# New prices in the planner's clock and an earlier high part of the weights, in a hybrid encoder layer on one Trainium2 core

## The chip, the cores and the metric

The kernel runs on one core of one Trainium2 chip. The time is device microseconds of one execution of the whole layer, from inputs in device memory to outputs in device memory. TensorE (PE) multiplies matrices, VectorE (DVE), ScalarE (ACT) and GpSimd (POOL) work on elements, and SyncE (SP) issues most of the transfers. Each engine executes its own list of instructions in the order in which the program wrote them, and waits on semaphores where it needs another engine's result.

## The reference

The layer is applied to two request groups, one sequence of 512 tokens and one of 1024, with one shared set of weights in float32 (width 1024). It has three sublayers, each with a normalization before and after, and shift, scale and gate from a conditioning vector:

```
x <- x + 1/2 * gate1 * norm(SwiGLU_1(mod(norm(x))))            # 1024 -> 2816 -> 1024
x <- x + gate2 * norm([pool_mixer(z_pool) | rwkv7_mixer(z_rwkv)] @ W_out),  z = mod(norm(x)) @ W_in
x <- x + 1/2 * gate3 * norm(SwiGLU_2(mod(norm(x))))
```

The RWKV mixer has 8 heads of 64, and runs a linear recurrence over the tokens in both directions:

```
S = S * decay_t + (S @ -kk_t) b_t^T + v_t k_t^T        # 64 x 64 a head, b = kk * a
y_t = S @ r_t
```

The two directions are added, normalized by head, given a bonus term and multiplied by a gate.

## The kernel before

**Blocks.** The 1536 tokens are three blocks of 512: blocks 0 and 1 are the long sequence, block 2 the short one. Activations stand with features on the 128 partitions and tokens along the free dimension.

**Dense layers.** A product in float32 accuracy is made of three products in the faster format float32r: weights and activations are each split into a high part and a low part, and `mm3` issues high x high, high x low and low x high. In names of the profile `whi` and `wlo` are parts of weights, `hh`/`hl` and `gh`/`gl` of activations, and `u`, `v`, `y` are accumulators in PSUM. One weight tile is 128 x 512 elements and serves 12 such products of 512 columns. The class `WStream` (line 483) feeds the tiles: `load` issues a transfer from device memory into one of five buffers `wraw`; `split` makes the high part (a copy by ACT) and the low part (a subtraction by POOL or DVE); `get`, called for each tile that is used, has tile i + 3 split and tile i + 8 loaded. While the scan runs (`scanning` is not empty), DVE makes every low part; otherwise POOL makes most of them.

**The scan.** The recurrence is computed in chunks of 64 tokens. Twelve macro steps, eight for the long sequence (group 1 of the code) and four for the short one, each hold two groups of four chunks in two directions (`gi` is 0 or 1). `scan_prep` makes decays and masked chunk matrices. `scan_inv` inverts triangular chunk matrices, for `gi` 0 by 62 dependent small DVE operations and for `gi` 1 by 62 dependent small POOL operations on the tile `XN`; before them stand two transposes on DVE (`XN<-MU`), and after them three (`MU<-XN` twice, `MU<-MU`), followed by 16 products of 32 x 32 on TensorE (`sM<-MU`), a copy by ACT and 16 more. The two inversions exclude each other. `scan_state` carries the state chunk by chunk, for each direction in three steps of a few products (`sb<-SBD,AR` and `sb<-MU`; `sb<-XN,MU`; `sb<-MU,BKt`, `sb<-AR,SBD` and `sb<-MU`), with copies by ACT between them and an update of the state `SBD` by DVE at the end. `scan_post` normalizes what is done.

**What runs beside what.** The main process goes through feed-forward 1 of blocks 0, 1 and 2, the input projections and the output projections, then feed-forward 2. The scan of the long sequence runs beside feed-forward 1 of block 2 (`mainC`) and what follows. The output projection of block 0 (`wout_gen`) needs the flag `("m", 1)`, which says that the long sequence's scan is done. Between layers, `post_gen` and `prenorm` (normalization after and before a sublayer, column tile by column tile, on DVE, ACT and POOL) make the inputs of the next dense layer. The projections of the pooled half (`wpool_gen`) are placed between them.

**What sets the order.** All of this is written as generators. The program that builds the kernel runs them one step at a time and notes an estimated clock (`Estimate`): for each engine the time at which it would be free, for each piece of each tile the time at which it would be ready. Every call on an engine passes through `Queue` (which is why all instructions have line L161 in the profile), and `Estimate.op` adds a price in nanoseconds to the engine's time. It prices the instruction by engine, operation and number n of elements a partition (or columns of a product, with k rows and m columns of the stationary operand), and holds the result ready for other engines `lat` later. `run_until` then picks, at TensorE's estimated time, the ready process of the smallest priority number. A process that yields `WAIT` is ready again some time after the result of its last instruction would be ready elsewhere, `AFTER_STATE` for priority 0 and `AFTER_OTHER` for the rest; one that yields `CHAIN` (the inversions) is ready `CHAIN_LEAD` before that result; one that yields `PIPE` (columns of `post_gen` and `prenorm`), 300 after it. The estimate exists only while the kernel is built. What remains of it is the order of the instructions on each engine. The choice of POOL or DVE for some operations (`pick`, `split`) is made by the same clock.

Of the kernel before, what the change touches and what calls it, by code (L numbers as in the profile page):

```python
# [10 lines left out]
F32R = mybir.dt.float32r  # L11
I32 = mybir.dt.int32
AF = mybir.ActivationFunctionType
# [4 lines left out]
P = 128  # L18
# [4 lines left out]
TB = 512  # L23
# [5 lines left out]
L2_EPS = 1e-12  # L29
WINDOWS = (2, 4, 8, 16)  # L30
PAD = 8
AFTER_STATE = 200
AFTER_OTHER = 400
CHAIN_LEAD = 300
PRIO_INV, PRIO_PREP, PRIO_POST, PRIO_NORM, PRIO_ZFIN = -0.5, -0.5, 0.8, 0, 0.9
POOL_LATE = 4000
OUT_AT = 7
# [4 lines left out]
class Estimate:  # L42
# [3 lines left out]
    def __init__(self):  # L46
        self.free = dict.fromkeys("VSGTY", 0.0)
        self.seen, self.rings, self.whole = {}, {}, set()
        self.last, self.table, self.moved = 0.0, None, 0.0

    def ring(self, t, key, bufs, whole=False):
        r = self.rings.setdefault(key, [])
# [34 lines left out]
    def op(self, e, name, args, kw):  # L87
        aps = [x for x in list(args) + list(kw.values()) if hasattr(x, "tensor") and hasattr(x, "offset")]
        out = kw.get("out", aps[0])
        n = 1  # L90
        for k in out.shape[1:]:
            n *= k
        t0 = self.free[e]
        boxes = [(self.box(x), x is out) for x in aps]
        for (nm_, p0, p1, f0, f1), w in boxes:
            for q in self.seen.get(nm_, ()):
                if q[0] < p1 and p0 < q[1] and q[2] < f1 and f0 < q[3]:
                    t = max(q[4], q[5] if w else 0.0)
                    t0 = max(t0, t + (0.0 if e == "T" else 130.0) if e == q[6] else t + q[7])
        lat = 150.0  # L100
        if name == "dma_start":
            cost, t = 60.0, max(t0 + 1700.0, self.moved)
            self.moved = t + n * out.shape[0] / 90.0
            lat = self.moved + 1400.0 - t0 - cost
        elif e == "S":
            f = str(args[2]) if len(args) > 2 else ""
            cost = 85 + 0.833 * n + (190 if hasattr(kw.get("scale"), "tensor") else 0)
            t = "e" if "Exp" in f else "s" if ("Silu" in f or "Tanh" in f) else self.table
            if t != self.table:
                cost += 1280  # L110
                self.table = t
        elif e == "V":
            cost = 65 + 1.04 * n + (60 if name == "scalar_tensor_tensor" else 0)
        elif e == "G":
            cost = {"memset": 50 + n, "tensor_scalar": 217 + 1.05 * n, "tensor_copy": 200 + 3 * n}.get(name, 100 + 2.2 * n)
        else:
            l = args[1]
            k, m = l.shape[0], 1
            for q in l.shape[1:]:
                m *= q  # L120
            if name == "transpose":
                cost = 125.0
            elif "32r" in str(l.dtype):
                cost = n / 2.35
            elif m <= 4:
                cost = 0.57 * n
            elif n >= 128:
                cost = 2.1 * n
            elif n >= 64:
                cost = 125.0 if k <= 64 else 190.0 if m > 64 else 78.0  # L130
            else:
                cost = 130.0 if m > 64 else 55.0
            lat = 200.0
        self.t0_ = t0
        t1 = t0 + cost
        self.free[e] = t1
        if name == "dma_start":
            e = "D"
        else:
            self.last = max(self.last, t1 + lat)  # L140
        for (nm_, p0, p1, f0, f1), w in boxes:
            l = self.seen.setdefault(nm_, [])
            if w:
                l[:] = [q for q in l if not (p0 <= q[0] and q[1] <= p1 and f0 <= q[2] and q[3] <= f1)]
                l.append((p0, p1, f0, f1, t1, 0.0, e, lat))
            else:
                l.append((p0, p1, f0, f1, 0.0, t1, e, lat))
            if len(l) > 48:
                del l[:16]
# [23 lines left out]
def encoder_kernel(ctx, tc, x_prompt, x_sample, c_prompt, c_sample, ada_w, ada_b, n1_pre, n1_post,  # L173
# [5 lines left out]
    V, S, G, T, SY = (Queue(est, *q) for q in (("V", nc.vector), ("S", nc.scalar), ("G", nc.gpsimd), ("T", nc.tensor),  # L179
                                               ("Y", nc.sync)))  # L180
# [3 lines left out]
    def nm(s):  # L184
        uid[0] += 1
        return f"{s}{uid[0]}"
# [15 lines left out]
    def mt(shape, tag, bufs, dt=F32, pool=None):  # L202
        return est.ring((pool or mp).tile(shape, dt, name=nm(tag), tag=tag, bufs=bufs), (id(pool), tag), bufs)
# [4 lines left out]
    class Proc:  # L208
        def __init__(self, gen, prio):
            self.gen, self.prio, self.ready, self.cond = gen, prio, est.free["T"], None  # L210
# [6 lines left out]
    def run_until(stop):  # L217
# [3 lines left out]
        while not stop():  # L221
# [27 lines left out]
            elif r == CHAIN:  # L249
                p_.ready = est.last - CHAIN_LEAD  # L250
            else:
                p_.ready = max(est.last + (AFTER_STATE if p_.prio == 0 else AFTER_OTHER), est.free["T"] + (0.0 if r == WAIT else r))

# [229 lines left out]
    class WStream:  # L483
        def __init__(self, items):
            self.items, self.raw, self.out = items, {}, {}
            self.i, self.nl, self.ns = 0, 0, 0

        def load(self, upto):
            while self.nl <= min(upto, len(self.items) - 1):
# [6 lines left out]
        def split(self, upto):  # L496
            while self.ns <= min(upto, len(self.items) - 1):
                self.load(self.ns)
                t = self.raw.pop(self.ns)
                wh = mt([P, TB], "whi", 5, F32R)  # L500
                wl = mt([P, TB], "wlo", 5, F32R)
                S.activation(wh, t, AF.Copy)
                now = est.free["T"]
                g_, v_ = max(now, est.free["G"]) + 1200, max(now, est.free["V"]) + 600
                E = G if not scanning and (g_ < now + POOL_LATE or g_ < v_) else V
                E.tensor_tensor(wl, t, wh.bitcast(F32), ALU.subtract)
                self.out[self.ns] = (wh, wl)
                self.ns += 1

        def get(self):  # L510
            i = self.i
            self.i += 1
            self.split(i + 3)
            self.load(i + 8)
            return self.out.pop(i)

    def cols(w, c0):
# [1111 lines left out]
```

## Time and profile before

| what | value |
|---|---|
| median of 3 runs | 3786.08 us (3785.57 to 3786.62) |
| profiled execution, its time | 3780.28 us |
| its span (first to last instruction) | 3778.3 us |
| TensorE busy | 3593.2 us, 95% of the span |
| VectorE busy | 1999.0 us, 53% |
| ScalarE busy | 1424.1 us, 38% |
| GpSimd busy | 1410.4 us, 37% |
| mean granted TensorE clock | 0.956 |
| read from device memory | 367.23 MB |

A row of a timeline gives start, duration, engine, operation, the tile written and the tiles read, shapes, count and, in brackets, idle time of the engine before it and what ended that. A row of a table by windows gives a stretch of time, then the busy time and the count of each engine in it, then the granted TensorE clock, the share of time in which the transfer engines were busy, and GB/s. A row of waits gives who waited for whom, microseconds in total, how often, and the longest.

### The profile page before, as it was taken

The page shows a single profiled execution, that of the slowest core. Times are in us where ns is not written, and L with a number is a line of the kernel's source. Part 1 is how long each engine was busy: PE and PEld are TensorE (multiplying, and loading weights), DVE is VectorE, ACT ScalarE, POOL GpSimd, SP SyncE. Part 2 cuts the span into 40 slices and gives each one's busy share as a digit, 9 for nine tenths or more (in the row PEclk, how much of TensorE's full clock was granted, in tenths as well). Part 3 has the DMA queues.
Part 4 walks back from the last instruction along what each step waited for, and adds up shares of the span by engine and source line. Part 5 has one row for each costly group of instructions (what it writes and reads, how often), then busy time and mean ns, then how long its engine had stood idle before and what let it go on. Part 6 is the DMA issues. An engine that isn't in the chain of part 4 may idle for free. (4 is left out here: it accounts for less than half of the span.)

```text
span 3778.3 us, 53665 instructions
## 1 busy us (share of the span) xinstructions
PE 3593.2 (95%) x19579; PEld 2703.6 (72%) x19579; DVE 1999.0 (53%) x3801; ACT 1424.1 (38%) x2776; POOL 1410.4 (37%) x1716
## 2 busy tenths in 40 slices
PE   7999999998999999999899989799999999999998
PEld 4667878876676767666666666567787778877886
DVE  3128362237237778776777776778448622242223
ACT  3324342225335434344345433343334432234222
POOL 2333444443132222234234233432344344444444
PEclk8999999998999999999889978599999999999999
DMA  7655343334344322222324343222254333334332
GB/s 274 235 181 169 91 154 92 99 90 134 123 128 126 93 67 88 82 71 87 117 76 122 96 137 105 74 73 77 87 159 151 103 115 98 93 109 132 94 95 78
DMA packets 557980, 432.11 MB, mean 114 GB/s; under 512 B 27029, under 2 KB 511572, under 8 KB 553620
## 3 DMA queue, kind: packets, MB, share of 16 engines
q1 hardware_dynamic: 524900, 379.90, 32.8%
q10 hardware_dynamic: 32816, 48.78, 4.1%
q8 instruction: 155, 2.54, 0.3%
q14 instruction: 109, 0.89, 0.1%
HBM read 367.23 MB, written 61.34 MB: 113 GB/s over the span
## 5 line engine op out<-in xcount | busy, mean ns | idle before, releaser
L161 POOL TENSOR_TENSOR wlo<-wraw,whi 128x512 fp32r<-128x512 f32 x672 | 892.6, 1346 | 1294.2 <-ACT whi L161 866.5
L161 DVE TENSOR_TENSOR y<-y,y 128x512 f32<-128x512 f32 x480 | 327.2, 684 | 848.9 <-PE y L161 847.9
L161 ACT ACTIVATE whi<-wraw 128x512 fp32r<-128x512 f32 x938 | 559.2, 622 | 181.6 <-PE v L161 139.7
L161 PE MATMUL u<-hh,whi 128*128 128x512 f32 x1392 | 568.2, 408 | 10.2 <-ACT zraw L161 4.0
L161 PE MATMUL u<-hl,whi 128*128 128x512 f32 x1392 | 564.3, 405 | 14.1 <-POOL hl L161 7.4
L161 PE MATMUL v<-hh,whi 128*128 128x512 f32 x1392 | 562.4, 404 | 12.8 <-ACT hh L161 7.6
L161 PE MATMUL u<-hh,wlo 128*128 128x512 f32 x1392 | 567.0, 407 | 0.1
L161 PE MATMUL v<-hl,whi 128*128 128x512 f32 x1392 | 561.0, 403 | 1.0 <-DVE hl L161 1.0
L161 PE MATMUL v<-hh,wlo 128*128 128x512 f32 x1392 | 560.7, 403 | 0.0
L161 PE MATMUL y<-gh,whi 128*128 128x512 f32 x1056 | 425.6, 403 | 12.8 <-DVE y L161 10.8
L161 PE MATMUL y<-gl,whi 128*128 128x512 f32 x1056 | 422.7, 400 | 0.2 <-DVE gl L161 0.2
L161 PE MATMUL y<-gh,wlo 128*128 128x512 f32 x1056 | 422.2, 400 | 0.0
L161 POOL TENSOR_TENSOR XN<-XN 64x126 f32<-64x126 f32 (+22 forms) x744 | 322.4, 433 | 93.6 <-DVE XN L161 18.5
L161 PEld LDWEIGHTS u<-hl,whi 128*128 128x128 f32 x1392 | 266.6, 191 | 81.5 <-DVE hl L161 12.6
L161 ACT ACTIVATE gh<-s 128x512 fp32r<-128x512 f32 x132 | 83.3, 631 | 639.3 <-DVE s L161 639.3
L161 PEld LDWEIGHTS u<-hh,whi 128*128 128x128 f32 x1392 | 266.3, 191 | 80.9 <-issue 7.7
L161 PEld LDWEIGHTS v<-hh,whi 128*128 128x128 f32 x1392 | 264.2, 190 | 82.9 <-ACT hh L161 11.3
L161 PEld LDWEIGHTS u<-hh,wlo 128*128 128x128 f32 x1392 | 266.3, 191 | 68.8 <-issue 9.5
L161 PEld LDWEIGHTS v<-hl,whi 128*128 128x128 f32 x1392 | 264.4, 190 | 66.3 <-issue 4.9
L161 PEld LDWEIGHTS v<-hh,wlo 128*128 128x128 f32 x1392 | 264.8, 190 | 62.9 <-issue 5.9
L161 DVE TENSOR_TENSOR wlo<-wraw,whi 128x512 fp32r<-128x512 f32 x266 | 206.4, 781 | 150.6 <-ACT whi L161 149.8
L161 PEld LDWEIGHTS y<-gh,whi 128*128 128x128 f32 x1056 | 199.9, 189 | 67.2 <-DVE y L161 12.0
(252 smaller groups left out, 4504.6 us busy)
## 6 DMA issues: line engine op xcount, KB each, us to landing
wraw<-in_f_w_dram SPq DMA_DIRECT2D x792, 256.0 KB
ada<-in_ada_w_dram SPq DMA_DIRECT2D x32, 1024.0 KB
wraw<-in_w_in_dram SPq DMA_DIRECT2D x98, 256.0 KB
xk<-xs ACTq DMA_DIRECT2D x96, 256.0 KB
xs<-y ACTq DMA_DIRECT2D x48, 256.0 KB
wraw<-in_w_out_dram SPq DMA_DIRECT2D x48, 256.0 KB
in_k<-zk SPq DMA_DIRECT2D x48, 128.0 KB
in_kk<-zkk SPq DMA_DIRECT2D x48, 128.0 KB
```

The source lines that it names most:

```text
L161: return f(*args, **kw)
```

## The change

It has two parts. In the first, the estimate's prices, its latency and three constants of the order are replaced. The latency from one engine to another goes from 150 to 380 (from TensorE, from 200 to 170), the extra charge of 130 for a dependence on the same engine goes, prices depend on more kinds of instruction, and TensorE gets a charge of 95 where a small product follows a dense one. In the second, `WStream` makes the high part in a function of its own: `get` has the high part of tile i + 3, the low part of tile i + 2 and the load of tile i + 7 issued.

```diff
-AFTER_STATE = 200
-AFTER_OTHER = 400
-CHAIN_LEAD = 300
+AFTER_STATE = 0
+AFTER_OTHER = 150
+CHAIN_LEAD = 500
...
-                    t0 = max(t0, t + (0.0 if e == "T" else 130.0) if e == q[6] else t + q[7])
-        lat = 150.0
+                    t0 = max(t0, t if e == q[6] else t + q[7])
+        lat = 380.0
...
-            cost = 85 + 0.833 * n + (190 if hasattr(kw.get("scale"), "tensor") else 0)
+            cost = 150 + 0.9 * n + (100 if hasattr(kw.get("scale"), "tensor") or hasattr(kw.get("bias"), "tensor") else 0)
...
-            cost = 65 + 1.04 * n + (60 if name == "scalar_tensor_tensor" else 0)
+            if name == "transpose":
+                cost = 100 + 1.8 * n
+            elif name == "tensor_tensor_scan":
+                cost = 150 + 2.0 * n
+            elif name == "tensor_scalar" or name == "tensor_copy":
+                cost = 150 + 0.75 * n
+            else:
+                cost = 150 + 1.04 * n + (60 if name == "scalar_tensor_tensor" and n <= 64 else 0)
         elif e == "G":
-            cost = {"memset": 50 + n, "tensor_scalar": 217 + 1.05 * n, "tensor_copy": 200 + 3 * n}.get(name, 100 + 2.2 * n)
+            cost = {"memset": 50 + n, "tensor_scalar": 217 + 1.05 * n, "tensor_copy": 200 + 3 * n}.get(
+                name, 200 + (2.1 if n > 256 else 1.65) * n)
...
             if name == "transpose":
-                cost = 125.0
+                cost = 120.0
             elif "32r" in str(l.dtype):
-                cost = n / 2.35
+                cost = 232.0 * n / 512
             elif m <= 4:
                 cost = 0.57 * n
+            elif n >= 256:
+                cost = (2.05 if k > 64 else 1.5) * n
             elif n >= 128:
-                cost = 2.1 * n
+                cost = 410.0 if k > 64 else 158.0
             elif n >= 64:
-                cost = 125.0 if k <= 64 else 190.0 if m > 64 else 78.0
+                cost = 130.0 if k > 64 else 150.0 if "SBD" in l.tensor.name else 204.0
+            elif n >= 32:
+                cost = 88.0
             else:
-                cost = 130.0 if m > 64 else 55.0
-            lat = 200.0
+                cost = 240.0
+            dense = "32r" in str(l.dtype)
+            if self.dense and not dense:
+                cost += 95.0
+            self.dense = dense
+            lat = 170.0
...
         def split(self, upto):
             while self.ns <= min(upto, len(self.items) - 1):
                 self.load(self.ns)
-                t = self.raw.pop(self.ns)
-                wh = mt([P, TB], "whi", 5, F32R)
+                self.high(self.ns)
+                t, wh = self.raw.pop(self.ns), self.hi.pop(self.ns)
                 wl = mt([P, TB], "wlo", 5, F32R)
-                S.activation(wh, t, AF.Copy)
...
+        def high(self, upto):
+
+            while self.nh <= min(upto, len(self.items) - 1):
+                self.load(self.nh)
+                wh = mt([P, TB], "whi", 5, F32R)
+                S.activation(wh, self.raw[self.nh], AF.Copy)
+                self.hi[self.nh] = wh
+                self.nh += 1
...
-            self.split(i + 3)
-            self.load(i + 8)
+            self.high(i + 3)
+            self.split(i + 2)
+            self.load(i + 7)
```

More of the change, by code (lines that the diff above doesn't have):

```diff
@@ L48, in __init__ @@
         self.seen, self.rings, self.whole = {}, {}, set()
-        self.last, self.table, self.moved = 0.0, None, 0.0
+        self.last, self.table, self.moved, self.dense = 0.0, None, 0.0, False
     def ring(self, t, key, bufs, whole=False):
@@ L485, in __init__ @@
             self.items, self.raw, self.out = items, {}, {}
-            self.i, self.nl, self.ns = 0, 0, 0
+            self.i, self.nl, self.ns, self.nh, self.hi = 0, 0, 0, 0, {}
         def load(self, upto):
```

## The prediction

> **What bounds the kernel now.** I read the page's head and its forty slices first. In fences of the page the last row is the granted TensorE clock in tenths.
>
> ```profile
> span 3778.3 us, 53665 instructions
> PE 3593.2 (95%) x19579; PEld 2703.6 (72%) x19579; DVE 1999.0 (53%) x3801; ACT 1424.1 (38%) x2776; POOL 1410.4 (37%) x1716
> PE   7999999998999999999899989799999999999998
> PEclk8999999998999999999889978599999999999999
> ```
>
> TensorE is the bound nearly everywhere, and its work does not change here: the same products are made in another order. An order can only give back, or add, time in which TensorE is idle or runs at a reduced clock. So the next view is busy time and clock by stage: dense layers, scan beside the sample feed-forward, the rest of the scan with its changes of layer, scan beside the last feed-forward, dense again.
>
> ```profile
> core 0: us, PE busy (x) PEld busy (x) DVE busy (x) ACT busy (x) POOL busy (x), PEclk, DMA share, GB/s
> 0.00:1171.00 1171.00, 1111.02 (x4878) 839.26 (x4879) 469.12 (x709) 421.90 (x698) 442.34 (x418) 0.98 0.46 147
> 1171.00:1770.00 599.00, 585.48 (x4152) 420.34 (x4151) 442.79 (x986) 254.82 (x563) 172.61 (x356) 0.99 0.29 85
> 1770.00:2450.00 680.00, 609.12 (x4099) 429.12 (x4099) 497.94 (x1109) 283.38 (x643) 246.91 (x439) 0.82 0.34 103
> 2450.00:2700.00 250.00, 248.16 (x1887) 175.77 (x1884) 169.92 (x385) 102.25 (x241) 67.30 (x140) 1.00 0.24 71
> ```
>
> As a measure of loss I take length less busy time times clock (an estimate; a busy TensorE is not at its peak). It gives 599 - 585.48 x 0.99 = 19 us in the first scan stage, 680 - 609.12 x 0.82 = 181 us in the second, and 2 us in the third. The planner's order is nearly perfect where dense work is plentiful; all that a better order can win lies between 1770 and 2450. Four stretches there hold most of it.
>
> ```profile
> 1855.00:1930.00 75.00, 62.09 (x371) 43.42 (x371) 53.35 (x106) 33.75 (x73) 43.16 (x77) 0.57 0.30 89
> 2160.00:2200.00 40.00, 33.80 (x236) 22.60 (x235) 29.86 (x60) 14.32 (x31) 23.57 (x39) 0.79 0.45 140
> 2235.00:2290.00 55.00, 47.95 (x316) 33.25 (x315) 34.27 (x74) 18.42 (x47) 32.12 (x68) 0.57 0.33 106
> 2360.00:2445.00 85.00, 64.39 (x388) 45.39 (x388) 62.73 (x126) 33.69 (x71) 44.50 (x73) 0.54 0.20 65
> ```
>
> By the same measure they lose 40, 13, 28 and 50 us. In the first and the last no dense product exists: post_gen and prenorm of one block run as a chain over DVE, ACT and POOL, and the scan alone feeds TensorE. In the third the output projection waits for the scan's first group (flag m, 1). The waits of TensorE and DVE over 1140 to 2700 (total, times, longest) show what is late:
>
> ```profile
> PE sM L161 <- DVE MU L161: 25.1, 21, 5.4
> PE sb L161 <- DVE SBD L161: 10.1, 11, 2.1
> DVE wlo L161 <- ACT whi L161: 134.6, 78, 5.5
> ```
>
> **The estimated clock, part by part.** The old prices are too short for TensorE. Here is a piece of its timeline (start, duration):
>
> ```profile
> 1394.99 0.43 PE L161 MATMUL sb<-SBD,AR 128*64 128x128 f32 x2
> 1395.35 0.44 PE L161 MATMUL sb<-MU 64*64 64x64 f32 x4
> 1395.72 0.43 PE L161 MATMUL sb<-SBD,AR 128*64 128x128 f32 x2
> 1396.09 0.44 PE L161 MATMUL sb<-MU 64*64 64x64 f32 x4
> 1396.46 0.50 PE L161 MATMUL u<-hh,whi 128*128 128x512 f32 x1
> 1396.79 0.40 PE L161 MATMUL u<-hl,whi 128*128 128x512 f32 x1
> 1397.03 0.40 PE L161 MATMUL u<-hh,wlo 128*128 128x512 f32 x1
> 1392.20:1428.10 35.90, 35.86 (x279) 25.42 (x276) 21.95 (x56) 12.57 (x31) 26.47 (x63) 1.00 0.30 89
> ```
>
> The first two steps of the two scan directions take 1396.46 - 1394.99 = 1.47 us. The old formulas price them 2 x (269 + 2 x 125) = 1.04 us, the new ones 2 x (410 + 2 x 204) = 1.64 us plus 0.10 for the change of kind. A dense product repeats every 0.24 us there (the old price is 0.218, the new 0.232). Priced instruction by instruction, the 279 instructions of the last row come to 31.1 us by the old formulas and 36.9 by the new, against 35.9 that passed. So the old plan ran about 1.15 times too fast, and everything planned behind another engine got that much slack unasked. The new plan has scale one, and the constants only keep their sums: 150 + 200 becomes 380 + 0, 150 + 400 becomes 380 + 150, 150 - 300 becomes 380 - 500. What is still priced too short now becomes a stall. One such chain is the inversion of the second group (scan_inv with gi = 1), 62 dependent POOL operations, then transposes on DVE, then 16 products on TensorE:
>
> ```profile
> 1392.22 29.97 POOL L161 TENSOR_TENSOR XN<-XN 64x31 f32<-64x31 f32 x62
> 1422.27 1.29 POOL L161 TENSOR_TENSOR pv<-pv,bq 128x512 f32<-128x512 f32 x1
> 1428.08 2.20 DVE L161 STREAM_TRANSPOSE MU<-XN 32x512 f32<-32x512 f32 x2
> 1430.31 0.70 DVE L161 STREAM_TRANSPOSE MU<-MU 32x512 f32<-32x512 f32 x1
> 1431.15 1.17 PE L161 MATMUL sM<-MU 32*32 32x32 f32 x32 [0.45 <-DVE MU L161]
> 1620.02 30.25 POOL L161 TENSOR_TENSOR XN<-XN 64x31 f32<-64x31 f32 x62
> ```
>
> Summed over the 62 lengths (5712 elements a partition), the old price is 62 x (100 + 130) + 2.2 x 5712 = 26.8 us, the 130 being the old charge for a dependence on the same engine. The new price drops it: 62 x 200 + 1.65 x 5712 = 21.8 us. The rows say 30.0 and 30.3. Old price times 1.15 is 31 us, which is why the transposes came 5.9 us after POOL had ended and TensorE waited only 0.45. In the new plan TensorE's products stand 21.8 + 0.38 + 3 x 1.02 + 0.38 + 0.15 = 25.8 us behind the start of the chain, while POOL and the transposes need 30.0 + 2.9 + about 0.1 = 33.0. The difference is 7.2 us. DVE stands at the transposes for that time, with the scan's state updates, low parts and sums queued behind; TensorE, which takes its products in order, stands at the 16 products. What DVE has queued ahead of the transposes anyway takes from it: 1428.1 less the 31 us after 1392.2 leaves 4.9 us here. I take 2.5, between none and this row, so 4.7 us a time; ends 7.2 and 2.3.
>
> A stall also costs clock. TensorE waited 1.90 us before this row, and the two windows show what followed:
>
> ```profile
> 1336.49 0.44 PE L161 MATMUL sb<-XN,MU 64*64 64x64 f32 x4 [1.90 <-ACT XN L161]
> 1335.00:1340.00 5.00, 3.50 (x23) 2.27 (x23) 3.77 (x11) 2.96 (x8) 0.00 (x0) 0.70 0.22 60
> 1340.00:1345.00 5.00, 5.00 (x24) 3.59 (x22) 3.74 (x12) 0.00 (x0) 0.00 (x0) 0.62 0.35 101
> ```
>
> A loss of 5 x 0.30 + 5 x 0.38 = 3.4 us of full-speed work, nearly twice the idle time itself. The Trainium skill ("TensorE: Matmul & The Clock Gate", Part 1) says that the clock halves after an idle window of some 3.4 us and returns after one busy window. By that rule a stall would cost one window at half speed, 1.7 us instead of 3.4, and the forecast would be 14 us lower; this trace disagrees in two ways, since 1.90 us of idling sufficed, and since between 1855 and 1930 the clock stayed at 0.57 with TensorE busy 62 of 75 us. The rows decide.
>
> There are 12 macro steps. I count eight beside plentiful dense work: 8 x (4.7 + 3.4) = 65 us, and four at 1.5 us where TensorE starves already: 6. **Term 1: +71 us** (ends 8 x (2.3 + 1.7) = 32 and 12 x (7.2 + 3.4) = 127).
>
> **Term 2:** the DVE transposes get true prices (two of 1.02 us where the old formula said 0.60), so stalls of the first group's inversion shrink. They are part of the 25.1 us above: -10 (0 to -25).
>
> **Term 3:** without the unasked slack the scan's own chain is shorter, so the wait for the first group in 2235 to 2290 shrinks: -20 of the 28 us lost there (0 to -28).
>
> **Term 4:** the chains of post_gen and prenorm are planned wider. A column of post_gen with its addition on POOL was planned 657 + 150 + 1226 + 150 + 511 + 150 + 300 = 3.14 us, and is now 682 + 380 + 1275 + 380 + 611 + 380 + 300 = 4.01. Two chains in the starved stretches, 8 columns each: 14 us, half covered by scan work that TensorE must do anyway: +8 (0 to +14).
>
> **The weights.** The copy to the high part keeps its place, three tiles ahead; the subtraction for the low part moves one tile later, and DVE no longer stands behind ACT for it: up to 134.6 us in the scan. TensorE felt little of it (10.1 us of waits for SBD), so **term 5** is -5 (0 to -15). Outside the scan POOL does it, one tile (12 x 0.232 = 2.8 us) later, with two tiles of products as cover; uncovered it would cost the 1.3 us of the operation per tile. Loads are issued with one tile less of lead: the high copy comes four tiles (11.1 us) behind its load where it came five (13.9 us). In the dense stages I cost this at nothing, the four tiles of products being the cover.
>
> The sum is 71 - 10 - 20 + 8 - 5 = **+44 us** on the profiled execution's 3780.28 (a span of 3778.3 and 2.0 around it), so 3824. The runs' median is 5.8 us above that execution: **3830**.
>
> **The rivals.** *Faster:* accurate prices put scan work where TensorE starves, and DVE is so loaded when the transposes come that POOL's misfit is absorbed. Half of the 131 us lost in the four stretches returns, with term 2: -66 - 10 = -76, or 3710. For it: prices that fit TensorE within 3%, and 134.6 us of DVE freed. Against it: in two of the four no dense product exists, whatever the clock says, and 19 us in the first scan stage leave nothing to win. It decides if DVE is over 7.2 us behind when it reaches the transposes. *Little changes:* the kept sums leave the order of state steps as it is, and terms 1 and 3 cancel: 3786. *Starved loads:* four tiles are too few in the first 285 us, where the big modulation weights share the queues. This row shows a tile late once already:
>
> ```profile
> PE u L161 <- ACT whi L161: 4.0, 1, 4.0
> 0.00:95.00 95.00, 72.80 (x327) 41.13 (x328) 36.87 (x84) 32.28 (x53) 24.65 (x69) 0.84 0.78 274
> ```
>
> Some 100 tiles pass there; one in ten late by 4 us is +40: 3870 with the forecast's terms. It decides where a load takes over 11.1 us.
>
> **How the numbers follow.** Forecast 0.47, its own range 3790 to 3890 from term 1's ends. Faster rival 0.33, and 0.07 for small gains (terms 2, 3, 5 without 1: -35, or 3751); little changes 0.08; starved loads 0.05. A measurement of this kernel can tell 0.2%, about 7.6 us, from no change. So faster 0.40, same 0.08, slower 0.52. The range runs from the faster rival, a little beyond, to the forecast's upper end: 3700 to 3890.
>
> **What would show it.** In the profile after: for term 1, idle time of DVE before MU transposes released by POOL XN (now nearly none) and waits of TensorE for DVE MU far above 25 us; low slices of the clock between 1171 and 1770, where there is none now. For term 2, stalls behind DVE's own inversions gone. For term 3, the output projection of block 0 not waiting. For term 5, DVE's 134.6 us gone. For the rival, a clock above 0.9 over the stage that has 0.82. I am wrong if transposes come after POOL has ended all the same.

## The result: slower by 2.2%, and the profile after

| | before | after |
|---|---|---|
| median | 3786.35 us | 3869.04 us (3863.27 to 3884.68) |
| ratio of the times | | 1.0224, 95% interval 1.0210 to 1.0239 |
| profiled execution's span | 3778.3 us | 3861.6 us |
| mean granted TensorE clock | 0.956 | 0.942 |

The profiled execution was the fastest of the four, at 3863.27 us, so the views of after show some 6 us less than the median. From the head of its page, and the clock in its forty slices:

```profile
span 3861.6 us, 53781 instructions
PE 3614.7 (94%) x19579; PEld 2735.6 (71%) x19579; DVE 1964.3 (51%) x3745; ACT 1430.4 (37%) x2778; POOL 1484.7 (38%) x1772
...
PEclk8999999999999999989887977979999999999999
```

TensorE executes the same 19579 instructions. A float32r product is one of them; a small product in float32 is two, as the row `sM<-MU` x32 of the prediction shows for 16 products. Its clock now has low slices in other places than before. The table by stage, with the columns of before's, shows where:

```profile
0.00:1171.00 1171.00, 1102.43 (x4832) 836.06 (x4833) 441.53 (x685) 418.12 (x691) 460.69 (x431) 0.97 0.46 146
1171.00:1770.00 599.00, 567.53 (x4069) 408.36 (x4068) 445.23 (x978) 250.81 (x555) 174.64 (x362) 0.93 0.26 79
1770.00:2450.00 680.00, 600.25 (x4146) 426.70 (x4144) 478.48 (x1076) 278.12 (x626) 214.34 (x417) 0.86 0.32 98
2450.00:2700.00 250.00, 224.31 (x1633) 158.88 (x1634) 168.31 (x394) 102.24 (x239) 78.86 (x146) 0.86 0.25 79
2700.00:3861.00 1161.00, 1120.18 (x4903) 905.56 (x4901) 430.70 (x615) 381.12 (x668) 556.15 (x418) 0.99 0.37 111
```

By the prediction's measure (length less busy time times clock) the first scan stage loses 599 - 567.53 x 0.93 = 71 us where it lost 19, the second 164 where it lost 181, the third 57 where it lost 2. The measure is good for finding a place, not for a sum: over all stages it would give more than the 83.3 us by which the span grew. Counts of TensorE's instructions are better for that. Before 2700 us the changed kernel has executed 4832 + 4069 + 4146 + 1633 = 14680 of them, the kernel before 15016. In both the last update of the scan's state begins at the same time (two answers, first of before, then of after; the last figure of the range):

```profile
L161 DVE SCALAR_TENSOR_TENSOR SBD<-sb,PL,s0p x24: 271/284/294, 2643.9 to 2692.7; 64x64 f32<-64x64 f32 x24
```

```profile
L177 DVE SCALAR_TENSOR_TENSOR SBD<-sb,PL,s0p x28: 274/284/292, 2602.7 to 2692.7; 64x64 f32<-64x64 f32 x28
```

So the scan did not become longer. Up to that point 336 instructions fewer were executed, 46 of them before 1171 us and 290 beside the scan, and they are executed afterwards: the last stage has 4903 and 1120.18 us of busy TensorE, against this row of before:

```profile
2700.00:3778.00 1078.00, 1039.39 (x4574) 839.12 (x4572) 419.25 (x613) 361.74 (x634) 481.27 (x364) 0.99 0.37 112
```

That is 81 us more busy time in 83 us more length. What took TensorE's time during the scan is seen in the waits of after, over 1140 to 2800:

```profile
DVE MU L177 <- POOL XN L177: 37.1, 8, 9.8
DVE wlo L177 <- ACT whi L177: 12.0, 7, 3.8
...
PE sM L177 <- DVE MU L177: 32.9, 17, 6.1
PE sb L177 <- DVE SBD L177: 23.6, 26, 3.3
```

DVE stands eight times at the transposes that follow POOL's inversion, 37.1 us in all. The two groups of instructions, of before and of after, show that this is new (behind the bar: idle time before them, and who ended most of it):

```profile
L161 DVE STREAM_TRANSPOSE MU<-XN 32x512 f32<-32x512 f32 x48 | 51.3, 1068 | 1.8 <-POOL XN L161 0.8
```

```profile
L177 DVE STREAM_TRANSPOSE MU<-XN 32x512 f32<-32x512 f32 x48 | 51.2, 1066 | 38.1 <-POOL XN L177 37.1
```

One of the eight, from the timelines of DVE and TensorE in after:

```profile
1527.49 2.08 DVE L177 STREAM_TRANSPOSE MU<-XN 32x512 f32<-32x512 f32 x2 [6.87 <-POOL XN L177]
...
1530.44 1.88 PE L177 MATMUL sM<-MU 32*32 32x32 f32 x32 [5.93 <-DVE MU L177]
```

and the windows of 5 us around it:

```profile
1525.00:1530.00 5.00, 0.00 (x0) 0.00 (x0) 2.45 (x3) 0.00 (x0) 1.91 (x8) 0.64 0.00 0
1530.00:1535.00 5.00, 4.56 (x39) 3.94 (x40) 4.27 (x8) 2.55 (x4) 0.00 (x0) 0.50 0.05 18
1535.00:1540.00 5.00, 5.00 (x46) 3.63 (x44) 4.99 (x5) 1.75 (x3) 0.00 (x0) 0.84 0.30 90
1540.00:1545.00 5.00, 5.00 (x32) 3.55 (x30) 2.92 (x8) 4.11 (x11) 1.48 (x2) 1.00 0.18 52
```

From 1524.5 to 1530.4 TensorE does nothing: POOL finishes its chain, then DVE transposes. DVE stands too, since the transposes are next in its list. Another 4.56 x 0.50 + 5.00 x 0.16 = 3.1 us are lost at the lower clock until it is back at 1.00. That is 9.0 us for this stall.

### The profile page after: what moved, and what is told of

Same layout as the page of the kernel before. It is cut to its first block, busy times and chain, and to the rows that moved or that the text cites. A ratio compares the mean times of both kernels' runs of the same rounds, so it can differ in the third digit from the quotient of the medians.

```text
span 3861.6 us, 53781 instructions
## 1 busy us (share of the span) xinstructions
PE 3614.7 (94%) x19579; PEld 2735.6 (71%) x19579; DVE 1964.3 (51%) x3745; ACT 1430.4 (37%) x2778; POOL 1484.7 (38%) x1772
## 5 line engine op out<-in xcount | busy, mean ns | idle before, releaser
L177 POOL TENSOR_TENSOR wlo<-wraw,whi 128x512 fp32r<-128x512 f32 x694 | 926.1, 1353 | 1187.0 <-ACT whi L177 697.4
L177 POOL TENSOR_TENSOR XN<-XN 64x126 f32<-64x126 f32 (+22 forms) x744 | 313.9, 422 | 219.3 <-DVE XN L177 153.3
L177 ACT ACTIVATE gh<-s 128x512 fp32r<-128x512 f32 x132 | 83.3, 631 | 668.4 <-DVE s L177 668.4
L177 PEld LDWEIGHTS y<-gh,wlo 128*128 128x128 f32 x1056 | 201.8, 191 | 48.7 <-DVE wlo L177 1.5
```

Of the source, the lines that this page charges most:

```text
L177: return f(*args, **kw)
```

## The experiments

The first theory is the prediction's: the price of POOL's inversion (21.8 us planned, 30.0 measured) makes the loss. The rivals are that the new prices as a whole, TensorE's above all, lose time, or that the weights do.

**The inversion's price alone.** The changed kernel, with one price put right: 62 x 270 + 2.3 x 5712 = 29.9 us for the chain. The new price also holds for the 24 additions `bq<-bq,ta` of 256 elements, 0.86 us instead of 0.62 each; in before they take 0.81.

```diff
-                name, 200 + (2.1 if n > 256 else 1.65) * n)
+                name, 200 + 2.1 * n if n > 256 else 270 + 2.3 * n)
```

> The changed kernel with one price raised: a POOL operation of at most 256 elements costs 270 + 2.3 n in the estimate (62 of them with 5712 elements come to 29.9 us, what the trace shows) instead of 200 + 1.65 n (21.8 us). Theory A (the short price of POOL's inversion is the main cause): waits of DVE MU for POOL XN fall from 37 us to under 5, and most of the 83 us returns, 3785 to 3815. Theory B (all unasked slack is gone, POOL's price is one case among many): the waits go but the time stays at 3840 to 3865. Theory C (the weights' part is the cause): no change, 3865.

Measured: 3803.31 us, ratio to before 1.0050 (1.0033 to 1.0066). Of the 2.24% that the change had cost, 1.74 points or 66 us are back. The waits and two stages of this kernel, from an execution of 3789.28 us, the fastest of its four:

```profile
DVE MU L177 <- POOL XN L177: 6.2, 5, 2.5
...
PE sM L177 <- DVE MU L177: 13.7, 10, 6.5
```

```profile
1171.00:1770.00 599.00, 580.57 (x4305) 418.99 (x4305) 475.83 (x1051) 264.44 (x588) 181.30 (x362) 0.99 0.28 83
...
2450.00:2700.00 250.00, 244.39 (x1668) 181.01 (x1666) 147.24 (x308) 104.29 (x230) 95.57 (x158) 0.92 0.27 82
```

DVE's wait shrinks from 37.1 to 6.2 us, where under 5 was expected, and the losses of the first and third scan stage from 71 and 57 to 24 and 25 us.

**A like misprice in the kernel before.** POOL loses the old charge of 130 ns for a dependence on itself, so that its chain is planned at 62 x 100 + 2.2 x 5712 = 18.8 us. The charge goes for every POOL operation that depends on another; 744 of the 1716 operations are those of the chains, and each engine keeps its number of operations.

```diff
-                    t0 = max(t0, t + (0.0 if e == "T" else 130.0) if e == q[6] else t + q[7])
+                    t0 = max(t0, t + (0.0 if e in "TG" else 130.0) if e == q[6] else t + q[7])
```

> The kernel before with one price lowered: POOL loses the charge of 130 for a dependence on itself, so its 62 operations are planned at 62 x 100 + 2.2 x 5712 = 18.8 us, or 21.6 at the scale of 1.15 of that plan, against 30 measured: the same shortfall as in the changed kernel, with everything else as before. Theory A (the short price of POOL's chain makes the loss by itself): 3835 to 3870, DVE waits for POOL XN of 25 us or more. If the shortfall costs only in the new plan, without its slack: 3780 to 3800.

Measured: 3876.11 us, 1.0241 (1.0219 to 1.0263), the whole loss without any of the other new prices, and a little above the expected range. Its waits, and its end of the scan:

```profile
DVE MU L161 <- POOL XN L161: 21.3, 8, 5.2
...
PE sM L161 <- DVE MU L161: 47.8, 23, 8.3
```

```profile
L161 DVE SCALAR_TENSOR_TENSOR SBD<-sb,PL,s0p x48: 275/284/291, 2603.2 to 2777.5; 64x64 f32<-64x64 f32 x48
```

DVE stands less than in the changed kernel, and less than the 25 us that were expected; TensorE stands longer, and here the scan itself ends 85 us later. A price that is too short by so much is thus enough for such a loss; in which stage it is paid depends on the rest of the order.

**The weights.** Three kernels: the changed one with the old `WStream`, the one before with the new `WStream`, and the first experiment's with the old `WStream`. The core of the edit that goes back:

```diff
-            self.high(i + 3)
-            self.split(i + 2)
-            self.load(i + 7)
+            self.split(i + 3)
+            self.load(i + 8)
```

> The changed kernel with the old order of high and low parts and loads; prices and constants stay new. Theories A and B: 3860 to 3880, the waits of DVE for the high copy back near 130 us and TensorE hardly slower. Theory C (low parts a tile later, or loads with less lead, cost the time): 3780 to 3800.

> The kernel before with the new order of high and low parts and loads only; prices and constants stay old. Theories A and B: 3770 to 3790, with DVE's waits for the high copy (134.6 us) nearly gone. Theory C: 3850 to 3870.

> The kernel of e1_pool_price with the old order of the weights. If the weights' part carries what is left over the kernel before: 3780 to 3795. If the prices carry it: 3800 to 3810.

| kernel | time | ratio to before |
|---|---|---|
| new prices, old weights | 3862.85 us | 1.0205 (1.0190 to 1.0220) |
| old prices, new weights | 3791.88 us | 1.0010 (0.9996 to 1.0025) |
| new prices with the inversion at 29.9 us, old weights | 3782.17 us | 0.9985 (0.9974 to 0.9996) |

The waits of DVE, first in the kernel with new prices and old weights, then with old prices and new weights:

```profile
DVE wlo L177 <- ACT whi L177: 123.7, 73, 6.5
```

```profile
DVE wlo L161 <- ACT whi L161: 9.0, 8, 3.2
```

The new order of the weights does what it says, since DVE's waits for the high parts go from over 120 us to about 10, and in none of these runs does it save time. It changes the time by +0.1% alone and by +0.2% beside the new prices (1.0224 against 1.0205), both within the intervals. Beside the corrected price it costs 0.65% (1.0050 against 0.9985, with intervals that do not meet), which is all that was left there over the kernel before. In the old weights' company the inversion's price is worth the whole loss: 3862.85 against 3782.17, 81 us.

**TensorE's prices, and the DVE transposes.** In the first kernel the changed one gets all the old prices of TensorE back, without the charge for a change of kind (the latency of 170 stays). In the second the kernel before gets the new price of a DVE transpose and nothing else.

```diff
-                cost = 232.0 * n / 512
+                cost = n / 2.35
...
-                cost = 410.0 if k > 64 else 158.0
+                cost = 2.1 * n
...
-            if self.dense and not dense:
-                cost += 95.0
```

```diff
-            cost = 65 + 1.04 * n + (60 if name == "scalar_tensor_tensor" else 0)
+            cost = 100 + 1.8 * n if name == "transpose" else 65 + 1.04 * n + (60 if name == "scalar_tensor_tensor" else 0)
```

> The changed kernel with the old prices of TensorE only (its latency, the charge for a change of kind and the products' prices); DVE, ACT and POOL stay new. The plan of TensorE runs some 1.15 times too fast again beside the scan. Theory B: the unasked slack is back, 3780 to 3810. Theory A: POOL's chain is planned 21.8 x 1.15 = 25 us, still 5 us short, 3820 to 3860, with DVE's waits for POOL XN between 10 and 30 us.

> The kernel before with the true price of the DVE transposes (100 + 1.8 n) and nothing else. Theory: TensorE's waits for DVE MU fall from 25 to about 15 us and the time to 3765 to 3780 (term 2 of the prediction, 10 us). Rival: every new order shifts other waits by as much, 3780 to 3800.

Measured: 3822.17 us with the old TensorE prices, 1.0098 (1.0083 to 1.0113). The plan that runs too fast gives about half of the loss back, though the inversion is still priced at 21.8 us. From this kernel's waits and stages:

```profile
DVE MU L169 <- POOL XN L169: 18.0, 6, 6.5
```

```profile
1171.00:1770.00 599.00, 585.00 (x3960) 424.76 (x3959) 434.54 (x943) 248.53 (x538) 151.50 (x296) 0.99 0.29 87
1770.00:2450.00 680.00, 604.16 (x4156) 432.89 (x4156) 496.10 (x1122) 271.20 (x629) 234.06 (x435) 0.79 0.33 100
```

The wait halves, the first scan stage loses 20 us as before the change, and the second loses 203. This fits the prediction's view that the old prices' error on TensorE hid errors on other engines. The run changes all of TensorE's prices at once, though, so that the slack is what helped is argued and not shown.

The transposes' price alone gives 3803.56 us, 1.0047 (1.0031 to 1.0064): slower, where a gain was forecast, and above the range of the expectation's rival too. From its waits and stages:

```profile
PE sM L161 <- DVE MU L161: 24.5, 16, 4.7
PE sb L161 <- DVE SBD L161: 20.4, 13, 3.2
```

```profile
1770.00:2450.00 680.00, 595.70 (x3995) 422.89 (x3995) 485.19 (x1086) 276.26 (x632) 240.45 (x445) 0.79 0.32 99
```

The waits for DVE MU stay (24.5 us, before 25.1), those for the state update double (20.4 against 10.1), and the stage with the starved stretches loses 209 us instead of 181.

**The slack put back.** The constants of before (200, 400, 300) with the new latencies and the corrected inversion, first with the new weights, then with the old, and then with still larger ones.

```diff
-AFTER_STATE = 0
-AFTER_OTHER = 150
-CHAIN_LEAD = 500
+AFTER_STATE = 200
+AFTER_OTHER = 400
+CHAIN_LEAD = 300
```

In the third kernel they are:

```diff
+AFTER_STATE = 400
+AFTER_OTHER = 700
+CHAIN_LEAD = 0
```

> The kernel of e1_pool_price (new prices, with POOL's chain priced as measured) with the three old constants 200, 400 and 300: each wait is planned 200 to 250 ns later. Theory B for what e1_pool_price left open, some 20 us over the kernel before (missing slack): 3775 to 3795. Rival (the rest is not slack, it lies in the order of the dense stages): 3795 to 3815.

> The changed kernel with the inversion's price at the measured 30 us, the constants 200, 400 and 300 of before, and the old weight stream. If what the corrected price and the slack give back adds up with the weight part's few us (3776.2 with slack and the new stream, 3782.2 with the corrected price and the old stream, 3791.9 for the new stream alone, against 3784 to 3787 before), it comes to 3765 to 3775. If all three only remove the same stalls, it stays at 3774 to 3784.

> As the run beside it, with the constants at 400, 700 and 0: some 250 ns more slack behind every state step and 300 ns behind each inversion. If stalls behind unpriced lateness still cost time, the clock rises and it comes out 5 to 15 us under the run beside it. If what remains is dense work missing in the starved stretches, the scan only gets longer: 0 to 20 us over it.

| kernel | time | ratio to before |
|---|---|---|
| 200, 400, 300, new weights | 3776.19 us | 0.9979 (0.9969 to 0.9988) |
| 200, 400, 300, old weights | 3782.61 us | 0.9987 (0.9976 to 0.9998) |
| 400, 700, 0, old weights | 3802.87 us | 1.0036 (1.0024 to 1.0049) |

The first is 0.2% faster than the kernel before. Two of its stages, and its waits:

```profile
1770.00:2450.00 680.00, 617.70 (x4268) 435.13 (x4267) 530.78 (x1195) 289.47 (x664) 233.18 (x424) 0.84 0.34 105
2450.00:2700.00 250.00, 245.19 (x1734) 182.12 (x1733) 156.30 (x329) 102.62 (x230) 91.44 (x155) 0.96 0.28 83
```

```profile
DVE MU L177 <- POOL XN L177: 16.6, 8, 6.4
...
PE sM L177 <- DVE MU L177: 4.6, 5, 1.7
```

The second scan stage loses 161 us, 20 less than before, and the third 15, 13 more. DVE stands eight times for POOL here too, 16.6 us in all, but hardly any of it reaches TensorE, which waits 4.6 us. The gains did not add up in the second kernel, and still more slack only cost time. The old constants give back 27 us with the new weights (3803.31 to 3776.19) and nothing with the old ones (3782.17 and 3782.61). So what is left once the inversion's price is right depends on the pairing of weights and constants, and no single cause is shown for it.

## Why the prediction was right, and where its sum was off

The forecast was 3830, slower. The measured 3869 is slower, within the forecast's own range, and 39 us above its centre. The first experiment splits that error. It is the change without the short price, so it measures terms 2 to 5 and whatever was costed at nothing: 3803.31 against 3783.96, +19 us, where the sum had -27. Term 1 is the difference to the changed kernel, 66 us, where the sum had 71.

**Term 1 (+71) held in mechanism, and its size came out near.** It took eight stalls of 4.7 us for DVE; the profile shows eight of 37.1 / 8 = 4.6 us. It took 3.4 us of clock for each; the stall shown lost 3.1. Correcting the one price gives back 66 us with the new weights and 81 with the old. Two details were off. The eight are not all beside plentiful dense work: four begin before 1770, four after, and single stalls run up to 9.8 us, longer than the 7.2 worked out. And the waits of TensorE for DVE MU, expected far above 25 us, are only 32.9. Added up along the timelines, the waits at the 16 products right behind POOL's inversions went from 5.5 us before to 20.0 after, and five of the eight stalls held TensorE up by over 1 us there, where the sum let all eight reach it with 4.7 us. That the total came near 71 is thus partly luck. These waits still mark the kernels with the whole loss: 22.9 us with the new prices and old weights, 34.7 with the misprice in the kernel before, and at most 5.3 in all other experiments. The waits for SBD, which rose by 13.5 us, mark nothing: the two kernels with constants of 200, 400 and 300, without a loss, have 20.1 and 29.1. By which ways the rest of the loss reaches TensorE was not measured.

**The unasked slack** is supported by the run with the old TensorE prices, in which the change with the same wrong price of the inversion costs about half (1.0098).

**Term 2 (-10) failed.** True prices for the transposes alone made the kernel 0.47% slower, some 18 us. The prediction took the 25.1 us of waits for what a better price would remove. By the timelines only 7.3 of them stand at the 16 products right behind DVE's own inversions, so less than the 10 was there to win; 5.5 stand behind POOL's, and the rest at other products. In the changed kernel the 7.3 fell to 4.0, with the transposes' price alone they came to 8.4, and other waits grew. Why an order that knows more comes out worse here is not settled.

**Term 3 (-20) failed in its effect.** The stretch from 2235 to 2290 loses less, but others appeared. Of after:

```profile
2000.00:2050.00 50.00, 35.43 (x271) 26.17 (x273) 38.38 (x107) 14.82 (x40) 9.98 (x8) 0.61 0.26 84
2050.00:2100.00 50.00, 35.11 (x229) 24.51 (x228) 30.09 (x57) 21.86 (x47) 30.00 (x67) 0.74 0.07 22
2100.00:2213.00 113.00, 111.45 (x675) 82.28 (x675) 61.58 (x141) 51.16 (x103) 10.35 (x33) 1.00 0.47 138
...
2235.00:2290.00 55.00, 44.06 (x327) 31.42 (x326) 48.15 (x113) 21.77 (x48) 17.30 (x42) 0.88 0.38 113
...
2500.00:2560.00 60.00, 44.72 (x257) 30.50 (x257) 44.62 (x88) 28.49 (x59) 34.30 (x57) 0.61 0.20 66
```

The old stretch loses 16 us in place of 28, though it does not hold the same work any more. From 2000 to 2100, 52 us are lost; then for 113 us POOL is nearly idle and dense work runs at full clock, and from 2500 to 2560 the next 33 are lost. One reason lies in the order of the work: the dense work came later. The first weight tile of the output projections is issued by SP at these times, before and after:

```profile
1767.01 0.37 SPq L161 DMA_DIRECT2D wraw<-in_w_out_dram  x1
```

```profile
1908.31 0.37 SPq L177 DMA_DIRECT2D wraw<-in_w_out_dram  x1
```

The output projections began 141 us later, so the changes of layer, in which only the scan feeds TensorE, fell elsewhere in the scan. This alone does not make the loss: the kernel with only the new weights issues that tile at 1822.6 us, 56 later than before, and loses 0.1%. The stage as a whole loses 17 us less than before, against the net 27 that terms 2 to 5 promised; how the missing gain divides among the terms is not known.

**Term 4 (+8)** was not separated from term 3 by any run.

**Term 5 (-5):** the waits went from 134.6 to 12.0 us, as forecast, and no run shows a gain from it: the weights' part changed the time by +0.1%, +0.2%, +0.65% and, beside the old constants, -0.1% (0.9979 against 0.9987), the last again within the intervals.

**The dense stages, costed at nothing, fell some 16 us behind.** In the window up to 560 us, 2311 instructions are executed where 2381 were, and 70 x 0.232 is 16 us, an estimate; at 1171 us the difference is 46. One stretch, before and after:

```profile
500.00:530.00 30.00, 26.35 (x107) 21.26 (x106) 19.05 (x31) 14.44 (x26) 12.05 (x9) 0.89 0.47 150
```

```profile
500.00:530.00 30.00, 19.35 (x84) 15.47 (x82) 24.48 (x32) 9.80 (x18) 16.79 (x11) 0.82 0.63 201
```

Here `post_gen` runs over DVE and POOL, and TensorE waits longer for its sum, of before and of after:

```profile
511.16 1.84 PE L161 MATMUL y<-ones,acc 128*128 128x1 f32 x8 [3.65 <-DVE acc L161]
```

```profile
526.11 1.84 PE L177 MATMUL y<-ones,acc 128*128 128x1 f32 x8 [8.59 <-DVE acc L177]
```

The lateness appears with the new weights alone and with the new prices alone, and not with the misprice or the transposes alone in the kernel before. Its cause stays open. It is not a loss in the end by itself: the fastest kernel of the experiments, at 0.9979, has executed 2306 instructions by 560 us.

**The rivals.** *Faster* needed DVE to be over 7.2 us behind when it reaches the transposes; it stood idle for them instead. Its other half, the stage with the clock of 0.82, came to 0.86 and gave back 17 of the 66 us it promised. *Starved loads* came near the time by chance only: the one late tile in the first 285 us is the one of before,

```profile
PE u L177 <- ACT whi L177: 4.0, 1, 4.0
```

with 4.0 us in both kernels. *Little changes* is what remains without the wrong price: 0.9985 to 1.0050.

## What to carry to other kernels

In a plan made from prices, errors that are common to all engines can cancel, and an engine's price must be looked at beside those of the others: putting most of them right exposed the one that was still 8 us short on a chain of 62, at 1.7 to 2.1% of the time. Price a chain by the time from its first start to its end, not by the durations of its instructions. Before trusting a new set of prices, list the longest chains between engines and compare planned and measured time for each. Ask which of the waits reach the engine that bounds the kernel; a DVE that stood for 37 us went with a loss of 66 us or more in one order here, and one that stood for 17 us with no loss in another. A slack of a few hundred nanoseconds behind a result cost nothing here, while twice that did.

## What was not expected of the hardware

**A chain on POOL takes longer than its instructions.** The group of the inversion's operations in before (busy, mean ns):

```profile
L161 POOL TENSOR_TENSOR XN<-XN 64x126 f32<-64x126 f32 (+22 forms) x744 | 322.4, 433 | 93.6 <-DVE XN L161 18.5 <-ACT ta L161 8.0 <-ACT sg L161 7.8
```

In the inversion of the prediction's row, from 1392 to 1422 us, the 62 durations come to 25.2 us and the idle time between them to 4.9: 80 ns from one dependent operation to the next, 30.1 us in all. Over the twelve inversions the durations average 322.4 / 12 = 26.9 us, so others take longer than this one. The formula of the change (21.8) is below even the durations. The Trainium skill ("Perfetto Trace Analysis", GPSIMD Engine Instruction) says to time GpSimd by the spacing of starts rather than by reported durations; 25.2 against 30.1 us agrees with that.

**DVE operations with both inputs in SBUF can take longer beside POOL.** From the timeline of before:

```profile
504.36 0.69 DVE L161 TENSOR_TENSOR y<-y,xk 128x512 f32<-128x512 f32 x1
...
504.98 3.49 POOL L161 TENSOR_TENSOR wlo<-wraw,whi 128x512 fp32r<-128x512 f32 x2 [3.20 <-PE v L161]
505.57 1.78 DVE L161 SCALAR_TENSOR_TENSOR y<-y,coef,rb 128x512 f32<-128x512 f32 x1
507.39 1.64 DVE L161 TENSOR_TENSOR y<-y,xk 128x512 f32<-128x512 f32 x1
```

The same addition takes 0.69 us and then 1.64, and POOL's two subtractions 1.75 each, where POOL's operation of that shape in the prediction's row took 1.29. The Trainium skill ("SBUF — State Buffer", Who interferes with whom) says that a DVE instruction with two SBUF inputs contends with a GpSimd instruction that reads SBUF, and these rows agree in kind. Not every overlap costs as much: of DVE's subtractions for low parts in before, between 1140 and 2800 us, the 81 listed singly that ran beside POOL for a quarter of their time or more took 0.92 us on average, the 138 without overlap 0.68. Neither set of prices knows of it. Whether it makes the 16 us above was not tried.

**A stall of 6 us cost no more clock than one of 1.9, in the one case of each that was looked at.** In the windows around 1530 full clock is back some 6 us after the first product, and the loss is 3.1 us, near the 3.4 of the prediction's row. The Trainium skill ("TensorE: Matmul & The Clock Gate", Part 1) says that full clock comes after a busy window of about 3.4 us, and that these windows run freely. An estimate from it is up to two windows at half clock, 6.8 us or a loss of 3.4, and the 3.1 of this trace lies within that; the prediction had read it as one window.
